# Seven products instead of eight in the first quad of round 1 and of the output

## The chip, the cores and the metric

The kernel runs on one core of one Trainium2 chip. The metric is the device time of the launch in microseconds. The kernel before was timed three times: 909.9, 910.4 and 913.95 us, median 910.4 us. Its profiled execution took 909.45 us by the same clock, and 907.7 us from its first to its last instruction (the span).

## What is computed

One layer of a hybrid decoder, on 2048 tokens of width 1024 with 16 learned tokens ahead of them, in float32 throughout:

```python
hn   = rms_norm(h, norm_g)                        # h: (1, 16 + 2048, 1024)
proj = einsum('bld,de->ble', hn, w_in)            # w_in: 1024 x 4096
cx, cb, cc, cg, q, k, v, rg = split(proj, 8)      # each 512 wide
conv_out = short_conv_branch(cx, cb, cc, conv_w) * silu(cg)      # 3 taps, depthwise
ret  = head_group_norm(retention_chunkwise(rotary(q) * 128**-.5, rotary(k), v), ret_norm_g)
mixed = concat([conv_out, ret * silu(rg)])        # 4 retention heads of 128, chunks of 128
y    = rms_norm(h + einsum('ble,ed->bld', mixed, w_out), final_g)[:, 16:]
```

Nearly all the arithmetic lies in the two projections, `hn @ w_in` and `mixed @ w_out`.

## The kernel before

**Quads.** Both projections are cut into quads: a 2 x 2 grid of 512-deep blocks on one operand by a 2 x 2 grid on the other. The stationary operand of a quad is four 128 x 512 tiles (a pair of 128-column groups of `w_in`, or in the output two 128-token rows of the mixed activations). The moving operand, held in SBUF over many quads, is a 1024 x 1024 matrix in four blocks of 512 x 512: the transposed tokens of one round (`x`, scaled by `norm1_g`), or `w_out`.

A quad is computed in one of two ways. `quad` (matmuls on line 208) forms seven block products in a Strassen-Winograd scheme; it needs seven moving operands, of which numbers 0, 1 and 5 are plain blocks and 2, 3, 4 and 6 are sums of blocks, and seven stationary operands, made from the four raw tiles by four additions on GpSimd (`stationary`). `quad_plain` (matmuls on line 258) forms the eight ordinary block products from the four plain blocks on both sides, with no additions.

**Splits.** A block product takes four 128-deep steps. In each, both float32 operands stand as a high and a low half, and three matmuls of 128 x 512 are issued: low weight by high moving, high by low, high by high. So a block product is 12 matmuls. A split (`split`) is two instructions: ScalarE casts the source to the high half (`mh`, `wh`), VectorE subtracts it from the source for the low half (`ml`, `wl`). `mhIJ` and `mlIJ` are the halves of moving operand I, step J; each has one buffer, so a new round's operand can be written only when the last matmul of the old one has read it. Weight halves go round in three buffers each.

**Rounds.** Tokens run in two rounds of 1024. A round is eight pairs of quads: four retention heads (quads K,V and Q,RG), then four convolution groups (CC,CX and CG,CB). Then the output runs eight quads (`pair`), two 128-token rows each. The moving operand is changed twice: from round 0 to round 1, and from round 1 to `w_out`. These are the two handovers of this document. While a round runs, `prepare` forms the sums for the next operand and stores them in DRAM (`sums_x`, `sums_w`).

**A handover before.** `moving` loads and splits the four plain blocks: 0, 1, 7 and 5, with block 7 in the buffers of operand 4. `plain_parts` splits the four raw weight tiles into the buffers of operand 3. `prepared(m, ..., (1, 3))` reads the sums 2 and 6. The first quad is `quad_plain`; after it `prepared(m, ..., (0, 2))` reads the sums 3 and 4, and the second quad is the first in seven products.

Instructions are issued in order on each engine. A scheduler that plans with a cost model set that order when the kernel was built, across quads; so the queue of an engine mixes the work of the old quad, the handover and the next quad. All DMAs are issued on SyncE.

Of the kernel before, what the change touches and what calls it, by code (L numbers as in the profile page):

```python
# [21 lines left out]
HB = 512  # L22
NR = 2
BLK = SEQ // NR
CH = HB // P
KH = KT // 2
# [7 lines left out]
SUMS = (3, 2, 4, 6)  # L34
# [34 lines left out]
def hybrid_trunk(ctx: ExitStack, tc: tile.TileContext, t, out: bass.AP, chunk_decay):  # L69
# [5 lines left out]
    nc = tc.nc  # L75
# [14 lines left out]
    def gen(name="g"):  # L90
        return sb.tile([P, HB + 16], F32, name=name, tag="g", bufs=GEN)[:, : 2 + HB]
# [96 lines left out]
                nc.sync.dma_start(dst[n, kt], a)  # L188
            yield

    def prepared(m, src, ns):

        for n in ns:
            for kt in range(KH):
                a = gen("t")[:, :HB]
                nc.sync.dma_start(a, src[n, kt])
                parts(m, SUMS[n], kt, a)

    def quad(w, m, take):

# [311 lines left out]
        nc.vector.tensor_tensor(out=a, in0=a, in1=table[:, 0, :], op=ALU.mult)  # L512
        add(nc.vector, a, a, rot[:, :w])

    def head(h, r, m, rot_t, f, blocks, ahead, first=(), between=()):


        between = iter(between)
# [15 lines left out]
        if len(first) > 0:  # L534
            quad_plain(first[0], m, take)
        else:
            quad(stationary(blocks), m, take)
        next(between, lambda: None)()
        q, sg = [None, None], [None, None]

# [14 lines left out]
                nc.scalar.activation(d, d, AF.Silu)  # L555
                sg[j] = d

        if len(first) > 1:
            quad_plain(first[1], m, take)
        else:  # L560
            quad(stationary(load_raw(w_loads(2 * h + 1))), m, take)
# [80 lines left out]
    def output(pair, m, final_g):  # L642
        d = mixed[pair // 2]
        loads = [
            lambda a, i=i, k=k: nc.sync.dma_start(a.rearrange("p (k c) -> p k c", k=KH), d[pair % 2, i, k])
            for i in range(2)
            for k in range(2)
        ]
        ys = [[None, None], [None, None]]
        ss = small.tile([P, 2, 2], F32, name="so", tag="so")  # L650
        for i in range(2):
            for j in range(2):
                y = gen("yo")[:, :HB]
                row = (2 * pair + i) * P
                nc.sync.dma_start(y, x[row : row + P, j * HB : (j + 1) * HB])
                ys[i][j] = y
        last = [None]

        def take(i, j, pp, c):
            y = ys[i][j]  # L660
            if c is not None:
                add(nc.gpsimd, y, y, c)
            last[0] = nc.vector.tensor_tensor(out=y, in0=pp, in1=y, op=ALU.add)  # L663
            junk = sb.tile([P, HB], F32, name="rot", tag="rot", bufs=1)
            nc.scalar.activation(junk, y, AF.Square, accum_out=ss[:, i, j : j + 1])
            if i == j:
                ys[i][j] = gen("z")[:, :HB]
                nc.gpsimd.tensor_tensor(out=ys[i][j], in0=y, in1=final_g[:, j * HB : (j + 1) * HB], op=ALU.mult)

        if pair == 0:  # L670
            w = plain_parts(loads)
            prepared(m, sums_w, (1, 3))
            quad_plain(w, m, take)
            prepared(m, sums_w, (0, 2))
        else:
            quad(stationary(load_raw(loads)), m, take)
        for i in range(2):
# [33 lines left out]
    def ahead(r, n):  # L711


        if n == 2 * NG:
            return None, lambda: None
        blocks = load_raw(w_loads(2 * n))
        if r == 0 and n < NG:
            k, v = meta_state(n, blocks)
            return blocks, lambda: meta_update(n, k, v)
        if r == 0:  # L720
            meta_carry(n - NG, blocks)
        return blocks, lambda: None
# [4 lines left out]
    for r in range(NR):  # L727
# [7 lines left out]
        if r == 0:  # L735
            w = [None] * 4
            loads = w_loads(0)

            def begin(half):
                for n in (half, 2 + half):  # L740
                    w[n] = plain_part(n, loads[n], FIRST_W)

            m, b = moving(
                load_x(r), gain_of, {(0, 0): lambda: begin(0), (0, KH - 1): lambda: begin(1), (0, KT - 1): normalise_meta}
            )
            first = [[p for a, p in w]]
            k0, v0 = meta_state(0, [a for a, p in w])
            first.append(plain_parts(w_loads(1)))
            load_tables()
            nc.sync.dma_start(cols, t["cols"])  # L750
            t3 = [a[:, i * HB : (i + 1) * HB] for a in (row_tile("t3") for _ in range(2)) for i in range(2)]
            t1 = [sb.tile([P, HB], F32, name="t1", tag="tc", bufs=COPIES) for _ in range(KH)]
            for kt in range(KH):
                b11, b21, b12, b22 = (b[n * KH + kt] for n in range(4))
                block_sums(b11, b12, b22, b21, t1[kt], t3[kt], gain_of(kt), gain_of(KH + kt))
                parts(m, 2, kt, b22)
                parts(m, 6, kt, b21)
            for _ in row_factors(0, f):
# [10 lines left out]
            between = (lambda: meta_update(0, k0, v0), rest)  # L769
            later = prepare(load_x(1), sums_x, gain_of)  # L770
        else:
            m, b = moving(load_x(r), gain_of)
            first = [plain_parts(w_loads(0))]
            load_tables()
            prepared(m, sums_x, (1, 3))
            between = (lambda: prepared(m, sums_x, (0, 2)),)
            later = prepare(load_w_out, sums_w)
        blocks = None
        for h in range(NG):
            blocks = head(h, r, m, rot_t, f, blocks, lambda: ahead(r, h + 1), *((first, between) if h == 0 else ()))  # L780
            if h > 0:
                next(later, None)
                next(later, None)
# [3 lines left out]
            for _ in range(3):  # L787
                next(steps, None)

    m, b = moving(load_w_out)  # L790
    final_g = row_tile("final_g")
    nc.sync.dma_start(final_g, t["final_g"].partition_broadcast(P))
    for pair in range(SEQ // (2 * P)):
# [39 lines left out]
```

## Time and profile before

| Engine | busy, us | share of the span | instructions |
|---|---|---|---|
| TensorE (PE), matmuls | 887.2 | 98% | 4407 |
| VectorE (DVE) | 707.1 | 78% | 1177 |
| ScalarE (ACT) | 405.1 | 45% | 807 |
| GpSimd (POOL) | 391.6 | 43% | 290 |

The profiled execution took 909.45 us; its span is 907.7 us, at a mean granted TensorE clock of 0.996. HBM moved 128 GB/s over the span.

In rows of the timeline the first number is the start in us from the begin of the span, the second the length, then engine, line, operation, tiles (out<-in) and shapes, how many were merged, and in brackets the idle time before and what ended it. A row of stretches (windows) gives for each engine its busy time and in brackets how many instructions touch the stretch, then the clock, the DMA share and the rate. Matmuls are pipelined: their rows overlap, so the time of one is read from start to start.

### The profile page before, as it was taken

To read this page: it belongs to the slowest core of one execution; us is meant where nothing else is said; L and a number is where in the kernel's file an instruction comes from. 1 tells how busy PE (TensorE), PEld (TensorE's weight loads), DVE (VectorE), ACT (ScalarE), POOL (GpSimd) and SP (SyncE) were. 2 spreads that over 40 slices of the span, in tenths; PEclk is the share of its full clock that TensorE was granted. 3 is DMA by queue.
4 is the path that set the end of the run, shared out by engine and by line. 5 is a ranking of instruction groups with operands and counts; after the bars stand their busy time and mean duration, and the time that the engine had idled before them with its cause. 6 is when DMAs were issued, how large, how long until landed. Compare 5 with 4: busy or idle time off the path is not lost.

```text
span 907.7 us, 12870 instructions
## 1 busy us (share of the span) xinstructions
PE 887.2 (98%) x4407; PEld 726.4 (80%) x4407; DVE 707.1 (78%) x1177; ACT 405.1 (45%) x807; POOL 391.6 (43%) x290
## 2 busy tenths in 40 slices
PE   8999999999999999999999999999999999999996
PEld 5778878787886777878888888888888888788885
DVE  6699898997665665799888999877767698866764
ACT  8762242424343534565333242433333374554553
POOL 0133142322434645343333323435646554778773
PEclk9999999999999999999999999999999999999999
DMA  9801451623142323564126362222131585555532
GB/s 332 264 3 47 140 163 51 206 82 98 43 149 61 105 82 117 194 236 139 47 67 200 93 204 89 56 59 81 58 93 48 185 284 184 172 183 164 173 108 93
DMA packets 76242, 116.94 MB, mean 129 GB/s; under 512 B 7632, under 2 KB 24336, under 8 KB 76176
## 3 DMA queue, kind: packets, MB, share of 16 engines
q1 hardware_dynamic: 76176, 116.11, 40.0%
q8 instruction: 35, 0.57, 0.3%
q14 instruction: 31, 0.25, 0.1%
HBM read 90.92 MB, written 25.17 MB: 128 GB/s over the span
## 4 chain that ended last, share of the span: by engine, by line
PE 81%; DVE 9%; DMA 3%; ACT 3%; issue 2%; POOL 1%; SPq 0%; POOLq 0%; ACTq 0%; DVEq 0%
PE pj L208 65%; PE pj L258 6%; DVE wl L111 2%; DVE ml L111 1%; PE ms L609 1%; PE ms L610 1%; PE ms L599 1%; DMA ra<-in_x 1%; PE ms L584 1%; PE ms L392 1%; PE ms L633 1%; PE ms L569 1%; PE ms L574 1%; ACT mh L102 1%; DMA ra<-in_w_in 1%
## 5 line engine op out<-in xcount | busy, mean ns | idle before, releaser
L208 PE MATMUL pj<-mh,wl 128*128 128x512 f32 x1008 | 400.6, 398 | 4.8 <-DVE wl L111 3.7
L208 PE MATMUL pj<-ml,wh 128*128 128x512 f32 x1008 | 393.6, 390 | 1.1 <-DVE ml L111 1.1
L208 PE MATMUL pj<-mh,wh 128*128 128x512 f32 x1008 | 393.5, 390 | 0.0
L99 ACT CAST wh<-ra 128x512 fp32r<-128x512 f32 x216 | 133.8, 620 | 306.9 <-PE pj L208 255.3
L208 PEld LDWEIGHTS pj<-mh,wl 128*128 128x128 f32 x1008 | 189.6, 188 | 49.1 <-issue 3.4
L208 PEld LDWEIGHTS pj<-mh,wh 128*128 128x128 f32 x1008 | 189.4, 188 | 39.9
L208 PEld LDWEIGHTS pj<-ml,wh 128*128 128x128 f32 x1008 | 189.8, 188 | 39.0 <-DVE ml L111 1.4
L111 DVE TENSOR_TENSOR wl<-ra,wh 128x512 fp32r<-128x512 f32 x216 | 180.8, 838 | 49.0 <-ACT wh L99 48.4
L111 POOL TENSOR_TENSOR ra<-ra 128x512 f32<-128x512 f32 x72 | 111.9, 1554 | 78.9 <-issue 35.0
L108 POOL TENSOR_TENSOR sa<-ra 128x512 f32<-128x512 f32 x36 | 54.8, 1522 | 119.8 <-DVE wl L111 54.9
L111 POOL TENSOR_TENSOR ra<-sa,ra 128x512 f32<-128x512 f32 x36 | 54.2, 1506 | 107.2 <-DVE wl L111 106.8
L215 ACT COPY tc<-pj 128x512 f32<-128x512 f32 x108 | 62.7, 580 | 0.1
L258 PE MATMUL pj<-mh,ml 128*128 128x512 f32 x128 | 48.6, 394 | 2.6 <-ACT kv L525 1.9
L258 PE MATMUL pj<-ml,mh 128*128 128x512 f32 x128 | 50.2, 392 | 0.1
L258 PE MATMUL pj<-mh,mh 128*128 128x512 f32 x128 | 50.0, 395 | 0.0
L622 POOL TENSOR_TENSOR rp<-rs,neg_half 128x4 f32<-128x4 f32 x16 | 20.5, 1279 | 56.0 <-DVE rs L108 55.7
L467 POOL TENSOR_TENSOR c<-c,tc 128x512 f32<-128x512 f32 x16 | 28.9, 1805 | 34.4 <-ACT tc L490 34.4
L467 POOL TENSOR_TENSOR c<-c,rr 128x512 f32<-128x512 f32 x16 | 30.1, 1879 | 24.8 <-DVE c L455 13.0
L663 DVE TENSOR_TENSOR yo<-pj,yo 128x512 f32<-128x512 f32 x32 | 22.0, 688 | 19.4 <-POOL yo L108 10.1
L111 DVE TENSOR_TENSOR ml<-t,mh 128x512 fp32r<-128x512 f32 x40 | 35.3, 922 | 1.4 <-ACT mh L99 1.4
L108 DVE TENSOR_TENSOR tc<-pj,tc 128x512 f32<-128x512 f32 x32 | 22.0, 686 | 18.0 <-PE pj L208 18.0
L99 ACT CAST wh<-sa 128x512 fp32r<-128x512 f32 x36 | 22.3, 619 | 28.6 <-PE pj L208 28.2
(129 smaller groups left out, 1131.4 us busy)
## 6 DMA issues: line engine op xcount, KB each, us to landing
ra<-in_w_in SPq DMA_DIRECT2D x128, 256.0 KB, 2.7
x<-in_xT SPq DMA_DIRECT2D x48, 256.0 KB, 5.0
ra<-in_x SPq DMA_DIRECT2D x32, 256.0 KB, 3.5
w<-in_w_out SPq DMA_DIRECT2D x32, 256.0 KB, 5.3
ra<-mixed SPq DMA_DIRECT2D x32, 256.0 KB, 2.7
yo<-in_x SPq DMA_DIRECT2D x32, 256.0 KB, 4.3
mixed<-qg SPq DMA_DIRECT2D x16, 256.0 KB, 2.3
sums_x<-x SPq DMA_DIRECT2D x16, 256.0 KB, 2.7
```

The source lines that it names most:

```text
L99: nc.scalar.copy(out=hi, in_=src)
L102: nc.scalar.mul(hi, src, scale)
L108: eng.tensor_tensor(out=out, in0=a, in1=b, op=ALU.add)
L111: eng.tensor_tensor(out=out, in0=a, in1=b, op=ALU.subtract)
L208: nc.tensor.matmul(bank, a[:, ks], b, start=first and kt == 0 and n == 0, stop=kt == KH - 1 and n == 2, skip_group_check=not first,)
L215: nc.scalar.copy(out=c, in_=bank)
L258: nc.tensor.matmul(banks[i], a[:, ks], b, start=half + kt + n == 0, stop=half == 1 and kt == KH - 1 and n == 2,)
L392: nc.tensor.matmul(four[i], meta_s[:, i % 2 * KH + kt, :], blocks[i][:, kt * P : (kt + 1) * P], start=kt == 0, stop=kt == KH - 1,)
L467: eng.tensor_tensor(out=out, in0=a, in1=b, op=ALU.mult)
L569: nc.tensor.transpose(tp[:, c * P : (c + 1) * P], k[j][:, c * P : (c + 1) * P], ident)
L622: nc.gpsimd.tensor_tensor(out=rp, in0=rs, in1=neg_half.rearrange("p (c a) -> p c a", a=1), op=ALU.pow)
L663: last[0] = nc.vector.tensor_tensor(out=y, in0=pp, in1=y, op=ALU.add)
```

## The change

Both handovers run their first quad in `quad`. A new function, `moving_prepared`, loads and splits the seven moving operands in the order 0 to 6, the plain ones from `x` or `w_out` and the sums from DRAM, and calls `stationary` for the quad's weights after operand 1. Block 7 and its four splits are gone, and so are the split weights in the buffers of operand 3 and the split of the reading of sums into two parts. In round 0 the raw weights of the coming quad are loaded ahead by `ahead`. Round 0's own first two quads stay in eight products.

```diff
-    def prepared(m, src, ns):
-
-        for n in ns:
+    def moving_prepared(load, sums, blocks, scale=None):
+
+
+        m = [[] for _ in range(8)]
+        plain = {0: (0, 0), 1: (1, 0), 5: (1, 1)}
+        for i in range(7):
             for kt in range(KH):
-                a = gen("t")[:, :HB]
-                nc.sync.dma_start(a, src[n, kt])
-                parts(m, SUMS[n], kt, a)
+                if i in plain:
+                    half, j = plain[i]
+                    k = half * KH + kt
+                    parts(m, i, kt, load(k, j), scale(k) if scale else None)
+                else:
+                    a = gen("t")[:, :HB]
+                    nc.sync.dma_start(a, sums[SUMS.index(i), kt])
+                    parts(m, i, kt, a)
+            if i == 1:
+                w = stationary(blocks)
+        return m, w
...
-            quad(stationary(blocks), m, take)
+            quad(w or stationary(blocks), m, take)
...
         if pair == 0:
-            w = plain_parts(loads)
-            prepared(m, sums_w, (1, 3))
-            quad_plain(w, m, take)
-            prepared(m, sums_w, (0, 2))
+            m[:], w = moving_prepared(load_w_out, sums_w, load_raw(loads))
+            quad(w, m, take)
...
         if n == 2 * NG:
-            return None, lambda: None
+            return load_raw(w_loads(0)) if r < NR - 1 else None, lambda: None
...
         else:
-            m, b = moving(load_x(r), gain_of)
-            first = [plain_parts(w_loads(0))]
+            m, w = moving_prepared(load_x(r), sums_x, blocks, gain_of)
             load_tables()
-            prepared(m, sums_x, (1, 3))
-            between = (lambda: prepared(m, sums_x, (0, 2)),)
+            first = between = ()
             later = prepare(load_w_out, sums_w)
...
-    m, b = moving(load_w_out)
+    m = []
```

What it does to the queues, at three places. In these rows a line number above 200 is 11 higher in the changed kernel than the same line before.

VectorE, late in the handover to round 1, before the change. `ml` are low halves of moving operands, `wl` low halves of weights; `tc` and `c` belong to the old convolution quad.

```order
L103 SCALAR_TENSOR_TENSOR ml53_3872<-x_3869,gain_69,mh53_3871 128x512
L467 TENSOR_TENSOR tc_3715<-tc_3715,rr_369 128x512
L111 TENSOR_TENSOR ml21_3909<-t_3906,mh21_3908 128x512
L111 TENSOR_TENSOR ml22_3915<-t_3912,mh22_3914 128x512
L111 TENSOR_TENSOR ml23_3921<-t_3918,mh23_3920 128x512
L111 TENSOR_TENSOR wl_4124<-ra_4114,wh_4123 128x512
L111 TENSOR_TENSOR wl_4128<-ra_4116,wh_4127 128x512
L111 TENSOR_TENSOR ml60_3927<-t_3924,mh60_3926 128x512
L467 TENSOR_TENSOR c_3621<-pj_3670,c_3621 128x512
```

And now, about the same place:

```order
L111 TENSOR_TENSOR ml30_3895<-t_3892,mh30_3894 128x512
L111 TENSOR_TENSOR wl_3837<-ra_3776,wh_3836 128x512
L108 TENSOR_TENSOR tc_3715<-pj_3717,tc_3715 128x512
L111 TENSOR_TENSOR ml31_3901<-t_3898,mh31_3900 128x512
L111 TENSOR_TENSOR ml32_3907<-t_3904,mh32_3906 128x512
L111 TENSOR_TENSOR ml33_3913<-t_3910,mh33_3912 128x512
L111 TENSOR_TENSOR wl_3841<-ra_3778,wh_3840 128x512
L111 TENSOR_TENSOR ml40_3919<-t_3916,mh40_3918 128x512
L478 TENSOR_TENSOR c_3621<-pj_3670,c_3621 128x512
```

Before, the first weight split here (`wl_4124`) serves the second new quad. Now the first (`wl_3837`) serves product 0 of the first new quad, and stands behind the splits of moving operands 0, 1, 2 and part of 3.

GpSimd at the same handover, before: the three rows that end the old quad's `c`, and the additions for the second new quad (`sa_4122`, `ra_...`), then those of the third.

```order
L467 TENSOR_TENSOR c_3621<-c_3621,tc_3683 128x512
L467 TENSOR_TENSOR c_3625<-c_3625,rr_369 128x512
L108 TENSOR_TENSOR sa_4122<-ra_4118,ra_4120 128x512
L111 TENSOR_TENSOR ra_4118<-ra_4114,ra_4118 128x512
L467 TENSOR_TENSOR c_3625<-c_3625,tc_3715 128x512
L111 TENSOR_TENSOR ra_4114<-sa_4122,ra_4114 128x512
L111 TENSOR_TENSOR ra_4116<-ra_4116,ra_4114 128x512
L108 TENSOR_TENSOR sa_4414<-ra_4273,ra_4275 128x512
```

And now:

```order
L108 TENSOR_TENSOR sa_3835<-ra_3780,ra_3782 128x512
L111 TENSOR_TENSOR ra_3780<-ra_3776,ra_3780 128x512
L478 TENSOR_TENSOR c_3621<-c_3621,tc_3683 128x512
L478 TENSOR_TENSOR c_3625<-c_3625,rr_369 128x512
L111 TENSOR_TENSOR ra_3776<-sa_3835,ra_3776 128x512
L111 TENSOR_TENSOR ra_3778<-ra_3778,ra_3776 128x512
L478 TENSOR_TENSOR c_3625<-c_3625,tc_3715 128x512
L108 TENSOR_TENSOR sa_4108<-ra_4104,ra_4106 128x512
```

The four additions in the handover are now those of the first new quad, and the second new quad's four (from `sa_4108`) follow behind them: four more in all.

GpSimd at the handover to the output, before (`yo` and `z` are the output's residual rows, `c` the old quad's):

```order
L467 TENSOR_TENSOR c_6857<-c_6857,tc_6947 128x512
L111 TENSOR_TENSOR ra_7382<-sa_7390,ra_7382 128x512
L111 TENSOR_TENSOR ra_7384<-ra_7384,ra_7382 128x512
L668 TENSOR_TENSOR z_7242<-yo_7109,final_g_7106 128x512
L668 TENSOR_TENSOR z_7303<-yo_7115,final_g_7106 128x512
L274 TENSOR_TENSOR rf_7355<-rs_v_7356,neg_half_72 128x1
```

And now:

```order
L111 TENSOR_TENSOR ra_7007<-sa_7063,ra_7007 128x512
L111 TENSOR_TENSOR ra_7009<-ra_7009,ra_7007 128x512
L108 TENSOR_TENSOR yo_6999<-yo_6999,tc_7229 128x512
L478 TENSOR_TENSOR c_6843<-c_6843,tc_6933 128x512
L679 TENSOR_TENSOR z_7248<-yo_6999,final_g_6996 128x512
L108 TENSOR_TENSOR sa_7365<-ra_7361,ra_7363 128x512
L108 TENSOR_TENSOR yo_7001<-yo_7001,tc_7262 128x512
L111 TENSOR_TENSOR ra_7361<-ra_7357,ra_7361 128x512
L108 TENSOR_TENSOR yo_7005<-yo_7005,tc_7277 128x512
L111 TENSOR_TENSOR ra_7357<-sa_7365,ra_7357 128x512
```

The first output quad now adds parts of products to the residual rows on GpSimd (three `yo` rows, which eight products did not need), and the additions for the second output quad stand between them.

More of the change, by code (lines that the diff above doesn't have):

```diff
@@ L513, in rotary, with head @@
         add(nc.vector, a, a, rot[:, :w])
-    def head(h, r, m, rot_t, f, blocks, ahead, first=(), between=()):
+    def head(h, r, m, rot_t, f, blocks, ahead, w=None, first=(), between=()):
         between = iter(between)
@@ L556, in take @@
                 sg[j] = d
-        if len(first) > 1:
+        if first:
             quad_plain(first[1], m, take)
@@ L769, in hybrid_trunk @@
             between = (lambda: meta_update(0, k0, v0), rest)
+            blocks = None
             later = prepare(load_x(1), sums_x, gain_of)
         else:
-            m, b = moving(load_x(r), gain_of)
-            first = [plain_parts(w_loads(0))]
+            m, w = moving_prepared(load_x(r), sums_x, blocks, gain_of)
             load_tables()
-            prepared(m, sums_x, (1, 3))
-            between = (lambda: prepared(m, sums_x, (0, 2)),)
+            first = between = ()
             later = prepare(load_w_out, sums_w)
-        blocks = None
         for h in range(NG):
-            blocks = head(h, r, m, rot_t, f, blocks, lambda: ahead(r, h + 1), *((first, between) if h == 0 else ()))
+            blocks = head(h, r, m, rot_t, f, blocks, lambda: ahead(r, h + 1), *((w, first, between) if h == 0 else ()))
             if h > 0:
```

## The prediction

> **What bounds the kernel now.** First the page's busy times, and its 40 slices for TensorE and VectorE, in tenths.
>
> ```profile
> PE 887.2 (98%) x4407; PEld 726.4 (80%) x4407; DVE 707.1 (78%) x1177; ACT 405.1 (45%) x807; POOL 391.6 (43%) x290
> ...
> PE   8999999999999999999999999999999999999996
> ...
> DVE  6699898997665665799888999877767698866764
> ```
>
> TensorE (PE) is busy from end to end, so over the whole kernel work taken from it is time won. But a VectorE share of 78% is an average: slices 18 and 19, and 33, read 9, and there the handovers lie. The stretches show it: the two handovers' splits, then a stretch of the output for comparison.
>
> ```profile
> 380.50:413.50 33.00, 32.40 (x144) 26.49 (x143) 33.00 (x42) 21.80 (x39) 15.36 (x8) 1.00 0.65 243
> 728.60:759.20 30.60, 30.53 (x135) 24.96 (x134) 30.60 (x42) 19.11 (x36) 17.38 (x8) 1.00 0.70 223
> ...
> 806.00:826.00 20.00, 20.00 (x90) 16.57 (x89) 12.07 (x18) 9.89 (x21) 14.72 (x13) 1.00 0.50 159
> ```
>
> The fourth group is VectorE: 33.00 of 33.00 us and 30.60 of 30.60, against 12.07 of 20 later. In both handovers VectorE is full without a gap, and TensorE just is not held up, because eight plain products need only half of the moving operands.
>
> **The price of a product.** TensorE's first quad in round 1 runs without a break from here to here:
>
> ```profile
> 395.98 0.39 PE L258 MATMUL pj<-ml,mh 128*128 128x512 f32 x1
> 396.20 0.39 PE L208 MATMUL pj<-mh,wl 128*128 128x512 f32 x1
> ...
> 398.92 0.39 PE L258 MATMUL pj<-mh,mh 128*128 128x512 f32 x1
> ...
> 416.60 0.39 PE L258 MATMUL pj<-mh,mh 128*128 128x512 f32 x1
> 416.83 0.39 PE L208 MATMUL pj<-mh,wl 128*128 128x512 f32 x1
> ```
>
> From 398.92 to 416.60 are 79 matmuls, the first and the last of them included: 17.68 / 78 = 0.227 us each, start to start, not the 0.39 that a row shows. A product of 12 costs 2.72 us, and two products are taken out: **5.4 us**, if TensorE stays fed. 17 matmuls of that quad ran ahead of the old one's last 12 (from 396.20), so without them the old quad ends at 398.92 - 17 x 0.227 = 395.1. From there the new quad needs the halves of operand and weight k at 395.1 + 2.72 k.
>
> **What VectorE takes.** Two rows give its pace when nothing disturbs it, one when something does, and the last ends the handover's splits:
>
> ```profile
> 380.50 2.44 DVE L103 SCALAR_TENSOR_TENSOR ml<-x,gain,mh 128x512 fp32r<-128x512 f32 x2
> 385.99 2.07 DVE L103 SCALAR_TENSOR_TENSOR ml<-x,gain,mh 128x512 fp32r<-128x512 f32 x3
> 390.26 1.88 DVE L111 TENSOR_TENSOR ml<-ra,mh 128x512 fp32r<-128x512 f32 x3
> 408.38 4.58 DVE L111 TENSOR_TENSOR ml<-t,mh 128x512 fp32r<-128x512 f32 x3
> 412.88 0.68 DVE L111 TENSOR_TENSOR wl<-ra,wh 128x512 fp32r<-128x512 f32 x1
> ```
>
> Three splits take 1.88 us, so 0.60 from start to start (1.88 less one of 0.68, halved), or 0.665 with the gain; the three at 408.38 take 4.58. What lies beside those is GpSimd:
>
> ```profile
> 379.39 2.34 POOL L467 TENSOR_TENSOR c<-c,rr 128x512 f32<-128x512 f32 x1 [1.36 <-DVE c L455]
> 388.07 1.72 POOL L467 TENSOR_TENSOR c<-c,tc 128x512 f32<-128x512 f32 x1 [6.34 <-ACT tc L490]
> 396.02 1.74 POOL L467 TENSOR_TENSOR c<-c,rr 128x512 f32<-128x512 f32 x1 [6.23 <-DVE c L467]
> 397.73 1.74 POOL L108 TENSOR_TENSOR sa<-ra 128x512 f32<-128x512 f32 x1
> 399.55 1.62 POOL L111 TENSOR_TENSOR ra<-ra 128x512 f32<-128x512 f32 x1
> 404.99 4.02 POOL L467 TENSOR_TENSOR c<-c,tc 128x512 f32<-128x512 f32 x1 [3.82 <-ACT tc L490]
> 408.97 1.73 POOL L111 TENSOR_TENSOR ra<-sa,ra 128x512 f32<-128x512 f32 x1
> 410.79 1.63 POOL L111 TENSOR_TENSOR ra<-ra 128x512 f32<-128x512 f32 x1
> ```
>
> The view of one tile, the low halves made from read sums, gives the shortest, the median and the longest split of the whole kernel in ns:
>
> ```profile
> L111 DVE TENSOR_TENSOR ml<-t,mh x40: 677/684/1783, 48.3 to 778.8; 128x512 fp32r<-128x512 f32 x40
> ```
>
> A split lasts 684 ns in the median and at most 1783: a GpSimd operation can hold it up by 1.1 us. From 380.50 to 412.96 are 40 VectorE instructions (42 touch the stretch, one at each edge): 24 x 0.60 + 16 x 0.665 = 25.0 us, and they took 32.5. The 7.4 us over fall to 8 GpSimd rows, **0.9 us each**. In the output's handover 40 instructions from 728.61 to 759.20 took 30.6 us for 24.0, again beside 8: 0.82.
>
> ```profile
> 728.61 1.28 DVE L111 TENSOR_TENSOR ml<-w,mh 128x512 fp32r<-128x512 f32 x2
> ...
> 753.90 5.30 DVE L111 TENSOR_TENSOR ml<-t,mh 128x512 fp32r<-128x512 f32 x6
> ```
>
> [...]
>
> [...]
>
> [...]
>
> **The change, part by part.** Removed at each handover: 12 matmuls, four splits of block 7, four of weights. Added: seven splits of weights. So VectorE has about as many instructions; ScalarE (21.80 of 33.00 us busy) covers its half of them and goes at nothing. SyncE's queue loses the four loads of block 7 at each handover; the four raw weight tiles go ahead of the moving blocks, in round 0 by `ahead`, and the sums 2 to 4 and 6 are read in one run instead of two. The rate over the same 33 us, slice by slice:
>
> ```profile
> GB/s 400 405 410 405 405 407 395 392 412 385 392 390 400 405 397 412 405 410 395 365 382 340 243 25 0 0 0 37 278 2 0 0 0 10 0 0 177 328 151 0
> ```
>
> At 405 GB/s a tile of 262,144 bytes takes 0.65 us, no more than VectorE's own pace, and the transfers ran out at 400 us, 13 us before VectorE's last split: they lead. So the DMAs go at nothing; were a sum late, its four tiles would come 4 x 0.65 = 2.6 us later. What changes is when VectorE's work is due, and that GpSimd has four additions more ahead of it.
>
> Round 1. In the changed order the low half of weight k is instruction 21, 26, 33, 36, 41, 45 and 48 after 380.50, with all of operand k's first steps before it; and 4, 6, 7, 7, 8, 8, 8 GpSimd operations are due by then (old `c` rows and the new additions, of which two must follow weights 0 and 1, whose tiles they overwrite). With 0.60 an instruction, 0.065 more for each gain split and 0.9 an addition, weight 0 is ready at 380.5 + 12.6 + 0.5 + 3.6 = 397.2, 2.1 late. Weight 1: 402.0, 2.1 behind the shifted 399.9. Weight 2: 407.1, 2.4 behind. Weight 3 in time, weight 4 0.5 behind, the rest in time. Stalls: **7.1 us**.
>
> Output. TensorE's rows there, with the stalls that end in them:
>
> ```profile
> 736.63 0.39 PE L208 MATMUL pj<-mh,wh 128*128 128x512 f32 x1
> 737.09 0.50 PE L258 MATMUL pj<-mh,ml 128*128 128x512 f32 x1
> ...
> 746.54 0.39 PE L258 MATMUL pj<-mh,mh 128*128 128x512 f32 x1
> ...
> 775.13 0.39 PE L208 MATMUL pj<-mh,wh 128*128 128x512 f32 x1
> 776.10 0.47 PE L208 MATMUL pj<-mh,wl 128*128 128x512 f32 x1 [0.58 <-DVE wl L111]
> 777.68 0.50 PE L208 MATMUL pj<-ml,wh 128*128 128x512 f32 x1 [1.12 <-DVE ml L111]
> ```
>
> At 746.54 the plain quad goes on behind the old one's last product; 17 of its matmuls ran ahead here too, so the old quad ends at 746.54 - 17 x 0.227 = 742.7. The low halves are instruction 17, 21, 27, 31, 36, 40 after 728.6, and for the next quad's product 0, which TensorE's order puts before product 6, instruction 47. GpSimd operations due: 4, 5, 6, 7, 9, 11, 13, since the `yo`, `z` and the second quad's additions now come in between. At 0.85 each the waits are 0, 0, 1.7, 0.5, 2.0, 1.4 and 3.2: **8.8 us**.
>
> What the stalls of before come to there, from start to start over 0.227: 0.23 at 737.09, 0.74 at 776.10 and 1.35 at 777.68: 2.3 us, for sums 3 and 4 split late, which are now split earlier: won.
>
> The sum: -5.4 - 2.3 + 7.1 + 8.8 = **+8.2 us** on the profiled execution's 909.45, so 917.65; taken as **917.5**. The median of the runs, 910.4, is 0.95 above that execution, within their spread.
>
> **The one unknown price** is what a GpSimd operation costs here. From below: at nothing, weight 2 of round 1 is 0.3 late, nothing else, and the sum is -5.4 - 2.3 + 0.3 = -7.4: 902. From above: at 1.1 each the same chains give 8.7 + 12.1, and +13.1: 922.5. At 0.5 they give 3.9 + 4.3, and +0.5. I take 0.9 and 0.85, measured in the very stretches that the change alters.
>
> **Rivals.**
>
> *VectorE is kept ahead, and the 5.4 us are won.* GpSimd's operations would have to wait for VectorE instead. Two rows are like that, 404.99 with 4.02 us, and this one:
>
> ```profile
> 734.96 5.03 POOL L467 TENSOR_TENSOR c<-c,tc 128x512 f32<-128x512 f32 x1 [3.90 <-ACT tc L490]
> ```
>
> There a run of splits went by while GpSimd stood. Against it: the other rows of 1.6 to 1.75 show GpSimd let in at the next split, and weights 2 to 6 are made from what it delivers. Price 0 to 0.3: 902 to 906.
>
> *A draw.* The additions fall half into waits that VectorE has anyway, for instance behind products whose results it takes. Price about 0.5: 908 to 913. For it: the stalls themselves make gaps in which GpSimd costs nothing. Against it: VectorE's queue was never empty in 33 us.
>
> *GpSimd becomes the bound of the first output quads.* Its stretch 806 to 826 is busy 14.72 of 20 already, and three `yo` rows and a full set of additions now come while it also ends the convolution. Should the second quad's weights be late too, by another 1.7 us for each of three operations, it is 5 more: 923 and over. It decides when the second output quad's weight 2, not its low halves, ends TensorE's wait.
>
> *That the change does not do what it says* is out: the order has 24 matmuls fewer on line 208 and 258 together.
>
> **How the numbers follow.** A difference under 0.5% (4.6 us) cannot be told from none here. VectorE bound as summed: 0.61, at 914 to 922, of which 0.04 lies within 0.5%. Won in full: 0.18. A draw: 0.15. GpSimd bound: 0.06. So faster 0.18, same 0.19, slower 0.63. The range reaches to both sides until about 0.2 is out: 905 to 923.
>
> **What would show it.** In the profile after: matmuls with line 219 in both handovers, waiting for `wl` or `ml`, some 7 us in the first 30 us of round 1 and 8 to 9 around the first two output quads; VectorE full in both; more low halves near 1.78 us. The forecast is wrong if TensorE runs through both handovers, or if what it waits for there is a DMA or ScalarE rather than VectorE.

## The result and the profile after

The changed kernel takes 923.4 us (median; 921.2 to 924.3), the kernel before beside it 910.9 us: the ratio is 1.0131, with a 95% interval of 1.0112 to 1.0150. So it is 12.5 us slower; the forecast was 8.2 us and 917.5. The time lies 0.4 us above the top of the stated range. The profiled execution has a span of 922.2 us, 14.5 more than the one of before.

The page's busy times after:

```profile
PE 887.3 (96%) x4383; PEld 723.1 (78%) x4383; DVE 704.2 (76%) x1178; ACT 407.1 (44%) x808; POOL 400.8 (43%) x301
```

The 24 matmuls are gone, VectorE has as many instructions as ever, and GpSimd has 11 more. The view of the stretches, for the handover to round 1 and for the output's:

```profile
380.50:413.50 33.00, 26.28 (x103) 19.76 (x102) 33.00 (x42) 23.12 (x42) 15.96 (x10) 0.95 0.73 254
740.00:785.00 45.00, 35.66 (x144) 27.24 (x143) 43.40 (x51) 27.77 (x55) 26.18 (x17) 0.96 0.65 206
```

In the first stretch VectorE is busy for 33.00 of 33.00 us with 42 instructions, exactly as before, and in the second for 43.40 of 45.00. What has changed is TensorE: 26.28 us of work instead of 32.40. And a column that read 1.00 before reads 0.95 and 0.96: the granted clock.

TensorE's own rows show both. The row where a product begins carries the wait in brackets; the rows behind two of the waits start 0.43 us apart instead of 0.23:

```profile
397.52 0.50 PE L219 MATMUL pj<-mh,wl 128*128 128x512 f32 x1 [0.60 <-DVE wl L111]
402.12 0.50 PE L219 MATMUL pj<-mh,wl 128*128 128x512 f32 x1 [1.58 <-DVE wl L111]
...
404.75 0.39 PE L219 MATMUL pj<-mh,wh 128*128 128x512 f32 x1
408.01 0.65 PE L219 MATMUL pj<-mh,wl 128*128 128x512 f32 x1 [2.87 <-DVE wl L111]
408.46 0.63 PE L219 MATMUL pj<-ml,wh 128*128 128x512 f32 x1
...
411.44 0.45 PE L219 MATMUL pj<-mh,wh 128*128 128x512 f32 x1
411.73 0.39 PE L219 MATMUL pj<-mh,wl 128*128 128x512 f32 x1
...
754.41 0.50 PE L219 MATMUL pj<-mh,wl 128*128 128x512 f32 x1 [0.99 <-DVE wl L111]
760.28 0.77 PE L219 MATMUL pj<-mh,wl 128*128 128x512 f32 x1 [2.85 <-DVE wl L111]
...
763.28 0.40 PE L219 MATMUL pj<-ml,wh 128*128 128x512 f32 x1
...
768.96 0.47 PE L219 MATMUL pj<-mh,wl 128*128 128x512 f32 x1 [1.64 <-DVE wl L111]
774.63 0.47 PE L219 MATMUL pj<-mh,wl 128*128 128x512 f32 x1 [2.71 <-DVE wl L111]
778.75 0.50 PE L219 MATMUL pj<-mh,wl 128*128 128x512 f32 x1 [1.12 <-DVE wl L111]
```

All eight waits end with a low half of weights from VectorE. A wait costs some 0.16 us more than its bracket says, since rows overlap: 408.01 less 404.75, less the normal 0.227, is 3.03 us. So products 0, 1 and 2 of round 1 lost 0.76, 1.75 and 3.03, 5.5 us in all, and the output's products 1, 2, 4, 5 and the next quad's 0 lost 1.15, 3.01, 1.80, 2.87 and 1.28, 10.1 us. Which product it is follows from the operand in TensorE's order. The slow rows come on top: 8 steps from 408.01 to 411.44 take 3.43 us instead of 1.82, and 7 steps from 760.28 to 763.28 take 3.00 instead of 1.59, 3.0 us together.

How a low half comes to be late is seen in the timeline of all engines ahead of 408.01:

```profile
405.72 1.59 POOL L478 TENSOR_TENSOR c<-c,tc 128x512 f32<-128x512 f32 x1 [1.90 <-ACT tc L501]
...
406.11 1.75 DVE L111 TENSOR_TENSOR wl<-ra,wh 128x512 fp32r<-128x512 f32 x1
...
408.01 0.65 PE L219 MATMUL pj<-mh,wl 128*128 128x512 f32 x1 [2.87 <-DVE wl L111]
```

The split starts 0.39 us after a GpSimd product and takes 1.75 us instead of 0.68; TensorE starts 0.15 us behind its end.

### The profile page after: what moved, and what is told of

Same layout as the page of the kernel before. It is cut to its first block, busy times and chain, and to the rows that moved or that the text cites. A ratio compares the mean times of both kernels' runs of the same rounds, so it can differ in the third digit from the quotient of the medians.

```text
span 922.2 us, 12850 instructions
## 1 busy us (share of the span) xinstructions
PE 887.3 (96%) x4383; PEld 723.1 (78%) x4383; DVE 704.2 (76%) x1178; ACT 407.1 (44%) x808; POOL 400.8 (43%) x301
## 4 chain that ended last, share of the span: by engine, by line
PE 79%; DVE 9%; ACT 4%; DMA 4%; issue 3%; POOL 1%; SPq 0%; POOLq 0%; DVEq 0%; ACTq 0%
PE pj L219 68%; DVE ml L111 2%; PE pj L269 2%; DVE wl L111 2%; DMA ra<-in_x 1%; PE ms L620 1%; PE ms L621 1%; PE ms L610 1%; ACT mh L102 1%; PE ms L595 1%; DMA ra<-in_w_in 1%; PE ms L403 1%; PE ms L644 1%; PE ms L580 1%; PE ms L585 1%
## 5 line engine op out<-in xcount | busy, mean ns | idle before, releaser
L219 PE MATMUL pj<-mh,wl 128*128 128x512 f32 x1064 | 424.9, 399 | 20.5 <-DVE wl L111 17.3
L219 PE MATMUL pj<-ml,wh 128*128 128x512 f32 x1064 | 416.5, 391 | 0.0
L219 PE MATMUL pj<-mh,wh 128*128 128x512 f32 x1064 | 416.5, 391 | 0.0
L219 PEld LDWEIGHTS pj<-mh,wl 128*128 128x128 f32 x1064 | 200.8, 189 | 70.7 <-ACT mh L99 8.7
L111 DVE TENSOR_TENSOR wl<-ra,wh 128x512 fp32r<-128x512 f32 x228 | 194.0, 852 | 53.6 <-ACT wh L99 53.2
L219 PEld LDWEIGHTS pj<-mh,wh 128*128 128x128 f32 x1064 | 200.6, 189 | 42.8
L219 PEld LDWEIGHTS pj<-ml,wh 128*128 128x128 f32 x1064 | 200.9, 189 | 39.9 <-issue 0.5
L633 POOL TENSOR_TENSOR rp<-rs,neg_half 128x4 f32<-128x4 f32 x16 | 20.5, 1280 | 56.2 <-DVE rs L108 56.0
L108 POOL TENSOR_TENSOR yo<-yo,tc 128x512 f32<-128x512 f32 x24 | 37.7, 1570 | 10.6 <-ACT tc L226 10.6
L679 POOL TENSOR_TENSOR z<-yo,final_g 128x512 f32<-128x512 f32 x16 | 26.9, 1683 | 11.4 <-DVE yo L674 11.4
L637 DVE TENSOR_SCALAR pm<-ms,mv,rp 128x128 f32<-128x128 f32 x64 | 21.9, 404 | 12.9 <-POOL rp L633 12.9
```

Source lines behind the costliest of these rows:

```text
L108: eng.tensor_tensor(out=out, in0=a, in1=b, op=ALU.add)
L111: eng.tensor_tensor(out=out, in0=a, in1=b, op=ALU.subtract)
L219: nc.tensor.matmul(bank, a[:, ks], b, start=first and kt == 0 and n == 0, stop=kt == KH - 1 and n == 2, skip_group_check=not first,)
L633: nc.gpsimd.tensor_tensor(out=rp, in0=rs, in1=neg_half.rearrange("p (c a) -> p c a", a=1), op=ALU.pow)
L637: nc.vector.tensor_scalar(out=y[:, cs], in0=o[:, cs], scalar1=mv[:, c, 0:1], scalar2=rp[:, c, :], op0=ALU.subtract, op1=ALU.mult,)
```

## The experiments

**Theory 1** is the prediction's: VectorE has no gap, and each GpSimd operation on SBUF tiles takes about 0.85 us from it. **Theory 2**: VectorE has too many instructions in that order, whatever GpSimd does. **Theory 3**: the weights' sums themselves come late out of GpSimd's queue, and VectorE is only the last to pass them on.

### One handover at a time

Round 1 with seven products, the output as before (the other kernel is the reverse):

```diff
-            m[:], w = moving_prepared(load_w_out, sums_w, load_raw(loads))
-            quad(w, m, take)
+            w = plain_parts(loads)
+            prepared(m, sums_w, (1, 3))
+            quad_plain(w, m, take)
+            prepared(m, sums_w, (0, 2))
```

> The first quad of round 1 runs in seven products as in the changed kernel, the first quad of the output in eight as before. The profiles put some 6.5 us of the changed kernel's 14.5 us longer span at the handover to round 1 and 7.9 at the output. If the two handovers lose independently, this kernel takes before + 6 to 7, so 916.5 to 918. If one place alone is at fault (the output, say, with what round 1 loses made good later), it is at 911 or at 923.

> The other half: the output's first quad in seven products, round 1 begins in eight as before. Independent losses: before + 7 to 8 less nothing, so 917 to 919, and the differences of this kernel and of the one with round 1 alone add up to the whole change's 12.5. One place alone: 911 or 923.

Round 1 alone: 917.4 us, ratio 1.0072 (1.0049 to 1.0096). The output alone: 917.1 us, ratio 1.0070 (1.0053 to 1.0088). Beside 910.8 us these are +6.6 and +6.4; their sum, 13.0, is the whole change's 12.5 within the intervals. Each handover loses for itself, and neither of them is worth doing this way.

### The additions taken out, and run for nothing

The first kernel has no additions for the two handover quads:

```diff
-                w = stationary(blocks)
+                w = bare(blocks)        # seven splits of the four raw tiles
```

> Left out of the computation: the four additions on GpSimd for the weights of the two handover quads; their seven splits are made from the four raw tiles, so that VectorE and ScalarE have the same number of instructions in nearly the same order. Theory 1 (a GpSimd operation takes 0.85 us from VectorE, which has no gap): 4 x 0.85 = 3.4 us less lateness at each handover, and with the stalls below 2 us TensorE's clock does not fall behind them (2.0 and 1.6 us): some 10 us less, 913. Theory 2 (VectorE's own count of instructions and their order makes the splits late): no change, 922 to 924. Theory 3 (the sums come late from GpSimd, whose own queue waits): as theory 1, 912 to 914.

The second kernel keeps GpSimd's four operations per handover, in time and size, but nobody reads what they make:

```diff
+        add(nc.gpsimd, s1, a21, a22)
+        sub(nc.gpsimd, s1, a11, a21)
+        sub(nc.gpsimd, s1, w[0][1].bitcast(F32), a21)
+        sub(nc.gpsimd, s1, w[1][1].bitcast(F32), a21)
+        return w + [parts(a) for a in (a11, a21, a21, a12, a22)]
```

> Left out of the computation: the results of the same eight additions. GpSimd still does four per handover, of the same size, the first two ready when the raw tiles have landed, the last two after the low halves of weights 0 and 1, as in the changed kernel, but into a tile that nobody reads; the seven splits are made from the raw tiles. VectorE's order is that of the changed kernel. Theory 1 (VectorE is held up while GpSimd runs): as the changed kernel, 921 to 924. Theory 3 (the sums come late): as without the additions, about 913. Theory 2 (VectorE's own count): 922 to 924, but then the kernel without additions is there too.

Without the additions: 915.8 us, ratio 1.0057 (1.0042 to 1.0073). With additions that nobody reads: 923.5 us, ratio 1.0148 (1.0131 to 1.0165), the changed kernel's time. This settles theory 3: late sums are not the cause, since here no split waits for one. The group of the products' first matmuls says the same in one line each; behind the bar stand busy time, the mean of one, and the idle time ahead of the group. Before:

```profile
L208 PE MATMUL pj<-mh,wl 128*128 128x512 f32 x1008 | 400.6, 398 | 4.8 <-DVE wl L111 3.7
```

After:

```profile
L219 PE MATMUL pj<-mh,wl 128*128 128x512 f32 x1064 | 424.9, 399 | 20.5 <-DVE wl L111 17.3
```

Without the additions, and with additions for nothing:

```profile
L231 PE MATMUL pj<-mh,wl 128*128 128x512 f32 x1064 | 424.2, 399 | 15.7 <-DVE wl L111 13.9 <-DVE yo L686 1.2 <-ACT tc L238 0.6
```

```profile
L237 PE MATMUL pj<-mh,wl 128*128 128x512 f32 x1064 | 425.2, 400 | 19.8 <-DVE wl L111 14.7 <-ACT mh L99 2.2 <-ACT tc L244 1.6
```

Idle time ahead of products: 4.8, 20.5, 15.7, 19.8 us. But 915.8 was above the 913 expected, and still 5 us above before, so a good part of the waiting was left. Theory 2 could live in that part.

### GpSimd kept out of the handovers altogether

```diff
-                mul(nc.gpsimd, cs[j], cs[j], rr[j])
-                mul(nc.gpsimd, cs[j], cs[j], c)
+                if g < NG - 1:
+                    mul(nc.gpsimd, cs[j], cs[j], rr[j])
+                    mul(nc.gpsimd, cs[j], cs[j], c)
...
-            if c is not None:
+            if c is not None and pair > 0:
                 add(nc.gpsimd, y, y, c)
```

and the second new quad's additions left out like the first one's.

> Left out of the computation, beside the additions for the two handover quads' weights: all else that GpSimd does in the handovers, that is the two products for the old convolution quad's c (last group of each round), the additions for the second new quad's weights, the three additions of parts to the first output quad's residual rows, and its gain (a copy on ScalarE in its place). VectorE's splits and their order stay. Theory 1 (what GpSimd takes from VectorE is all that makes the splits late): by the sum of the prediction with GpSimd at nothing the splits are 0.3 us late, so 5.4 us of products and 2.3 us of old stalls are won: 903 to 905. Theory 2 (VectorE's count and order are the rest of it): the 4.9 us that the kernel without the eight additions still stands above before stay, 913 to 916.

904.5 us, ratio 0.9940 (0.9918 to 0.9962): inside the 903 to 905 of theory 1, and at the prediction's lower bound of 902 but for 2.5 us. VectorE's instructions in the handovers are the same splits in nearly the same order. The stretches and the group:

```profile
380.50:413.50 33.00, 31.07 (x134) 24.48 (x133) 32.34 (x53) 25.32 (x45) 0.00 (x0) 1.00 0.79 283
728.60:775.00 46.40, 45.19 (x198) 36.83 (x198) 40.36 (x63) 34.97 (x69) 9.13 (x7) 1.00 0.72 256
```

```profile
L231 PE MATMUL pj<-mh,wl 128*128 128x512 f32 x1064 | 422.8, 398 | 6.9 <-DVE wl L111 4.2 <-ACT tc L238 1.7 <-ACT wh L99 0.9
```

VectorE does 53 instructions in the 33 us in which it did 42 before and after the change, and still has 0.66 us to spare; TensorE's clock is at 1.00. In the second stretch GpSimd's 9.13 us begin at 761.17, with the second output quad. Theory 2 falls: without GpSimd VectorE feeds the seven products. What this kernel leaves out is work of the layer, so its time is not one that the layer could have.

### The costs by themselves

A kernel that computes nothing of the layer runs the disputed pieces one after the other, each stretch kept apart from the next; in short form:

```diff
+    both(24, a)             # VectorE alone: lo = a - b
+    both(24, a); gps(8)     # beside eight GpSimd additions
+    # 24 subtractions, and 3 GpSimd additions of results 2, 8 and 14
+    both(24, bank); gps(8)  # a in PSUM
+    one_in(24); gps(8)      # tensor_scalar, one SBUF input
+    # then matmuls with rests of 1 to 6 ScalarE copies
```

> Not this computation at all: the disputed costs by themselves, in stretches that are separated from each other. VectorE's subtraction of two SBUF tiles alone, GpSimd's addition alone, both side by side with GpSimd's eight back to back, VectorE with three single GpSimd additions, VectorE with one input in PSUM beside GpSimd, VectorE with one SBUF input beside GpSimd; then matmuls with rests of 1 to 6 ScalarE copies, once and five times in a row. Theory 1: 24 subtractions alone take 14.5 us (0.60 each), beside three single additions some 2.5 us more (0.85 each), with PSUM or one input no more than alone. Against it would be 14.5 us in all of these. On the clock: if it takes one rest of some 2.8 us, only the long rests are followed by matmuls of 0.43 us; if short rests in a row do it as well, the runs with five rests of 1.2 to 2.4 us show them too.

The timeline of VectorE, one row a stretch:

```profile
6.71 14.54 DVE L40 TENSOR_TENSOR lo<-a,b 128x512 fp32r<-128x512 f32 x24 [6.71 <-SPq L51]
31.33 23.06 DVE L40 TENSOR_TENSOR lo<-a,b 128x512 fp32r<-128x512 f32 x24 [10.07 <-SPq L55]
54.44 17.74 DVE L61 TENSOR_TENSOR wide<-a,b 128x512 fp32r<-128x512 f32 x24
72.34 14.44 DVE L40 TENSOR_TENSOR lo<-bank,b 128x512 fp32r<-128x512 f32 x24 [0.15 <-SPq L64]
86.92 16.66 DVE L44 TENSOR_SCALAR lo<-a 128x512 fp32r<-128x512 f32 x24
```

and GpSimd's in its first two:

```profile
21.38 9.80 POOL L48 TENSOR_TENSOR so<-c,d 128x512 f32<-128x512 f32 x8 [20.94 <-SPq L53]
31.37 13.44 POOL L48 TENSOR_TENSOR so<-c,d 128x512 f32<-128x512 f32 x8 [0.19 <-SPq L55]
```

Alone 24 subtractions take 14.54 us. Eight GpSimd additions beside them add (23.06 - 14.54) / 8 = 1.07 us each, and three single ones (17.74 - 14.54) / 3 = 1.07. With one input in PSUM the 24 take 14.44 us beside eight additions, no longer than the SBUF form alone; that form was not run without GpSimd. So the price per operation is 1.07 us where it meets a subtraction of SBUF tiles. The prediction took 0.85 to 0.9 from the kernel; that some operations there met another kind of instruction would explain the difference, but it is not shown. GpSimd pays too: its eight additions take 13.44 us instead of 9.80.

A GpSimd addition alone takes 9.80 / 8 = 1.22 us here, and VectorE loses 1.07 us to it, nearly its whole length.

### Work made ahead

GpSimd's additions for the handover quads were moved several quads earlier, with their results stored and read as raw tiles. This kernel and the five below compute the whole layer.

```diff
+            if h == NG - 1:
+                sum_ahead(*((mixed_loads(0), first_w) if r else (w_loads(0), first_x)))
```

> The whole computation, in the changed kernel's way, but the four sums of the weights of each handover quad are formed by GpSimd several quads earlier (after the last head of the round), stored, and read as raw tiles in the handover. That is the kernel without the eight additions (915.8) as a correct one, with eight tiles more to store and to read: theory 1 expects 914 to 917, and the same stalls in the handovers. If the additions cost as much where they are done now, it is back at 921 to 924.

913.7 us beside 908.8, ratio 1.0056 (1.0041 to 1.0071): the same ratio as without the additions. Earlier, they cost nothing that can be seen.

Next, the moving sums were stored as split halves, and read straight into the operands' buffers.

```diff
...
-                    parts(m, i, kt, a)
...
+                    nc.sync.dma_start(hi.bitcast(F32), sums[SUMS.index(i), kt, 0])
+                    nc.sync.dma_start(lo.bitcast(F32), sums[SUMS.index(i), kt, 1])
```

> The whole computation. While a round runs, the sums for the next moving operand are not only formed but also split, and both halves are stored; in the handover the halves of operands 2, 3, 4 and 6 are read straight into their buffers. That takes 16 of VectorE's some 47 instructions out of each handover (16 x 0.60 = 9.6 us) and puts them where VectorE has gaps; GpSimd's work stays. If VectorE is what binds, with or without GpSimd, its lateness of 2 to 6 us from product 2 on is gone, the first two products stay some 2 us late together: 911 - 5.4 - 2.3 + 2 x 2 = 907, between 904 and 909. Rival: the transfers bind, since a handover now reads 12 + 32 + 4 tiles of 0.65 us, 31 us, and each read of a half stands in the queue until the old quad leaves its buffer: 912 to 918.

> As the kernel that stores the sums' halves (922), with the sums formed and split beside the convolution groups instead of the heads, and operand 5 split ahead of operand 4. In that kernel the handovers were nearly free of stalls, and TensorE lost some 8 us in the rounds instead, waiting for VectorE beside the heads, where it is nearly full. If that is the reason, those 8 us go, and 912 to 914 is left; a stall or two fewer at operand 5 may take it to 909. If the extra work costs the same wherever it lies, 920 to 923.

> Both: the halves of the moving sums and the weights' sums of the two handover quads are made ahead, beside the convolution groups. VectorE then has 16 instructions fewer in each handover and GpSimd four fewer. Theory 1: the handovers run without stalls of more than 1 us each, 911 - 5.4 - 2.3 = 903, with some 2 to 4 us for the first two products and for the work in the rounds: 904 to 909. If the work beside the convolution groups makes TensorE wait there, 912 or more.

All three came out slower than before, far from the 904 to 914 us hoped for: 922.0, 926.1 and 926.2 us, ratios 1.0114, 1.0185 and 1.0183. Of the expectations' second branches (912 to 918, 920 to 923, 912 or more) only the last covers its time. The handovers did as expected: the first new quads' waits shrank. The rounds did not. Beside the heads and beside the convolution groups alike, TensorE waits for VectorE where it did not before, or not as long; a row of the first kernel and one of the second:

```profile
564.70 0.79 PE L224 MATMUL pj<-mh,wl 128*128 128x512 f32 x1 [2.46 <-DVE kv L108]
```

```profile
273.82 0.26 PE L444 MATMUL ms<-ident,mk 16*128 16x16 f32 x1 [4.27 <-DVE mk L442]
```

A likely reason, argued and not shown apart, is that sixteen more splits in a stretch of the rounds meet chains in which TensorE waits for VectorE within a few us, and VectorE's average of 76% says nothing of those. TensorE's clock has its part: up to the last matmul, the granted clock falls to one half in four places of the first trace, four of the second and three of the third, against one place before; its mean over each trace is 0.991, 0.990 and 0.988, against 0.996. Whether a finer spreading would do it was not tried.

The last pair keeps to what worked. In the first kernel the weights' sums of the second quads are made ahead as well; in the second, the old convolution quad's four products for `c`, in the last group of each round, also go from GpSimd to VectorE.

```diff
-                mul(nc.gpsimd, cs[j], cs[j], rr[j])
-                mul(nc.gpsimd, cs[j], cs[j], c)
+                eng = nc.gpsimd if g < NG - 1 else nc.vector
+                mul(eng, cs[j], cs[j], rr[j])
+                mul(eng, cs[j], cs[j], c)
```

> The whole computation. As the kernel with the weights' sums of each handover quad made ahead (913.7), and the same for the second quad of each, so that GpSimd's last work in the handovers is the old convolution quad's two products for each c, the residual rows and their gain. The second quad's additions fall partly into the handover when the first quad's are gone: theory 1 expects up to 2 us less, 911 to 914.

> As the kernel before it in this list, with the four products for c of each round's last convolution group on VectorE instead of GpSimd. VectorE gets four instructions more in each handover, 4 x 0.60 = 2.4 us. Theory 1 with the price measured apart (1.07 us taken from VectorE by one GpSimd operation): 4 x (1.07 - 0.60) = 1.9 us less per handover although VectorE has more to do, 0 to 4 us faster than its neighbour, 907 to 912, level with before or a little faster. Theory 2 (VectorE's count binds): up to 4.8 us slower than its neighbour, 915 to 919.

With the products on GpSimd: 912.8 us, ratio 1.0026 (1.0008 to 1.0045). With them on VectorE: **908.6 us, ratio 0.9974 (0.9957 to 0.9990)**, 2.1 us faster than before. VectorE was given eight instructions more and the kernel became 4.2 us faster: no count of VectorE's instructions explains that, and it is the clearest sign for theory 1. The same two stretches, first with the products on GpSimd, then on VectorE:

```profile
375.00:415.00 40.00, 37.59 (x160) 29.12 (x158) 39.16 (x57) 28.91 (x51) 12.11 (x8) 1.00 0.81 282
740.00:785.00 45.00, 41.78 (x175) 33.44 (x174) 40.75 (x52) 26.94 (x53) 22.91 (x15) 0.96 0.70 233
```

```profile
375.00:415.00 40.00, 37.88 (x162) 29.77 (x161) 39.89 (x65) 28.35 (x51) 1.31 (x3) 1.00 0.81 288
740.00:785.00 45.00, 42.03 (x183) 33.89 (x182) 39.52 (x55) 26.98 (x55) 26.94 (x16) 1.00 0.73 236
```

VectorE gets 65 instructions done in 40 us instead of 57, and in the output TensorE's clock stays at 1.00. Part of the 4.2 us is that clock: over the runs of each kernel its mean is 0.9945 and 0.9963, a difference of 0.0018 or some 1.6 us of 910. That it follows from the shorter waits alone is not shown.

## Why the prediction was right, and where it failed

**The bound and the sign** held; the time did not, since 923.4 lies outside the range. VectorE fills both handovers, the new waits sit where they were forecast, and they end with VectorE's low halves. The three rivals fell: VectorE is not kept ahead, the additions do not fall into waits that are there anyway (taking them out gives 7.6 us), and GpSimd's queue is not what is waited for (additions for nothing cost as much). That this last rival was given 923 us and over, the time that was measured, is chance.

**The gain of two products**, 5.4 us, was not measured by itself. Without GpSimd in the handovers the kernel is 5.7 us faster than before, which fits it; but GpSimd's work is left out there too, and by the prediction's sum it would have been 7.4.

**The chain of splits**, instruction by instruction: weights 0, 1 and 2 of round 1 were put at 397.2, 402.0 and 407.1; the products began at 397.52, 402.12 and 408.01. The waits were forecast at 7.1 and 8.8 us, 15.9 together, and came to 5.5 and 10.1, 15.6 together. That the sum came out is luck, since the errors cancel: single waits were off by up to 1.9 us. The output's waits began a product earlier than forecast, and product 0 of round 1 waited 0.76 and not 2.1, because the old quad itself ended later, behind a wait at its product 5 that grew. That product's row before, and after:

```profile
389.49 0.50 PE L208 MATMUL pj<-mh,wl 128*128 128x512 f32 x1 [0.60 <-ACT tc L215]
```

```profile
390.04 0.68 DVE L111 TENSOR_TENSOR wl<-ra,wh 128x512 fp32r<-128x512 f32 x1
390.86 0.47 PE L219 MATMUL pj<-mh,wl 128*128 128x512 f32 x1 [1.59 <-ACT mh L99]
```

The bracket names ScalarE. But the tile named is a moving half of the new quad, which the old one does not read, and a split of the old quad's weights ended on VectorE at 390.04 + 0.68 = 390.72, 0.14 us ahead of the matmul, as at 408.01. In the kernel with additions for nothing the same place waits 1.00 us, and there the bracket names `wl` on VectorE. So it is most likely VectorE once more, already late within the old quad, where the prediction's chains do not look.

**The step that failed** is the sum: it prices the waits and sets what comes behind them at nothing, without a reason. Two of the eight waits were followed by matmuls at half speed, for 3.4 and 3.0 us, and 1.6 and 1.4 us were lost. The terms as they were measured: -5.4 - 2.3 + 15.6 + 3.0 for the clock + 1.0 for the old quad's wait = +11.9. They come from the profiled execution, whose span is 14.5 us longer; the medians differ by 12.5. Of the 2.6 us that are left, 0.9 is a wait for ScalarE in the middle of round 1, at 703.57, which before does not have, and most of the rest is delays of 0.25 us and less around the waits.

Nor does a higher price per operation do it. At 1.1 us, near the 1.07 measured apart, the prediction's chains give 922.5, close to the measured time, but by way of 20.8 us of waits where 15.6 were seen.

The profile of before had the effect of the clock, in a place that the change does not touch; a wait, and behind it matmuls at 0.42 to 0.58 us from start to start:

```profile
121.31 0.48 PE L420 MATMUL ms<-mk 16*128 16x128 f32 x2 [2.13 <-DVE mk L108]
...
123.34 0.78 PE L208 MATMUL pj<-mh,wl 128*128 128x512 f32 x1
123.92 0.63 PE L208 MATMUL pj<-ml,wh 128*128 128x512 f32 x1
124.34 0.63 PE L208 MATMUL pj<-mh,wh 128*128 128x512 f32 x1
```

TensorE ran at half speed behind this wait of 2.13 us and behind those of 2.87 and 2.85 us in the changed kernel, so whoever forecasts new waits of that length has to price what comes behind them.

## What to carry to other kernels

An engine that is full without a gap can have a price list for its neighbours: here one GpSimd operation on SBUF tiles cost VectorE, at subtractions of two SBUF tiles, 1.07 us, more than the 0.60 of such a subtraction, and with eight products moved from GpSimd to VectorE the kernel took 908.6 us instead of 912.8. Before an edit moves due times closer together, write down for each operand the instruction number at which it is ready and add the neighbours' price; that found seven of the eight waiting products here, each wait to within 2 us. Then allow for half speed behind a wait that leaves TensorE idle for most of 3.4 us (1.6 and 1.4 us were lost behind two of the eight here), and if an edit loses, look for what can leave the tight stretch, not only for what can be undone.

## What the hardware showed that was not expected

**Half speed behind waits, by a grid and not by one length.** In the kernel of pieces, 40 matmuls behind a rest of 1.38, 2.03, 2.68 and 3.33 us, then 12 behind rests of 1.38 and of 2.03 us in a row:

```profile
130.52 9.37 PE L76 MATMUL acc<-m,w 128*128 128x512 f32 x40 [1.38 <-ACT m L81]
141.92 9.37 PE L76 MATMUL acc<-m,w 128*128 128x512 f32 x40 [2.03 <-ACT m L81]
153.96 10.96 PE L76 MATMUL acc<-m,w 128*128 128x512 f32 x40 [2.68 <-ACT m L81]
168.25 10.89 PE L76 MATMUL acc<-m,w 128*128 128x512 f32 x40 [3.33 <-ACT m L81]
...
228.70 3.02 PE L76 MATMUL acc<-m,w 128*128 128x512 f32 x12 [1.38 <-ACT m L81]
...
269.60 4.61 PE L76 MATMUL acc<-m,w 128*128 128x512 f32 x12 [2.03 <-ACT m L81]
```

A single rest of 2.03 us costs nothing behind it, one of 2.68 us costs 1.6; but rests of 2.03 us with 3 us of work between them cost 1.6 us each (4.61 against 3.02). In the layer's kernels the length alone does not decide it either. The wait of 2.13 us at 121.31 has slow rows behind it before; the same wait in the kernel with round 1 alone, at 120.83, has none.

The granted clock in the traces shows the pattern. It falls to one half for 3.41 us at a time, at times for two or three such stretches in a row, and within a trace all of them lie on one grid: in the changed kernel they begin at 121.41, 408.13 and 759.70 us, 84 and 103 times 3.413 us apart. In the stretch of the grid ahead of each one TensorE was busy for at most 2.13 of 3.41 us, mostly for far less: for 1.28, 0.54 and 1.14 us in the changed kernel. Three of the grid in the changed kernel; the clock is the column ahead of the last two:

```profile
404.72:408.13 3.41, 0.54 (x3) 0.15 (x2) 3.41 (x5) 3.12 (x6) 1.59 (x1) 1.00 0.10 29
408.13:411.54 3.41, 3.41 (x9) 2.63 (x10) 3.41 (x6) 0.10 (x1) 0.46 (x1) 0.50 0.60 154
411.54:414.96 3.42, 3.42 (x17) 2.80 (x16) 3.42 (x4) 1.11 (x2) 2.46 (x2) 1.00 0.00 0
```

A wait is shared out between the stretches of the grid that it touches. In the kernel without additions a wait of 3.03 us, up to 757.50, falls half into one and half into the next, and nothing follows; in the one with round 1 alone two waits of 0.42 and 0.73 us fall into one, and half speed follows at 785.50:

```profile
752.67:756.09 3.42, 1.81 (x8) 1.15 (x7) 3.42 (x3) 2.78 (x6) 3.42 (x3) 1.00 0.57 171
756.09:759.50 3.41, 2.00 (x9) 1.66 (x10) 3.41 (x5) 0.81 (x3) 0.98 (x2) 1.00 0.31 102
```

```profile
782.09:785.50 3.41, 2.10 (x8) 1.16 (x8) 3.41 (x4) 1.17 (x3) 2.20 (x2) 1.00 0.35 115
```

Over all the traces here, between the first 8 us and the last matmul (in the kernel of pieces from its first matmul on), each of the 35 stretches with TensorE busy for 1.50 us or less was followed by half speed, and none with 2.14 us or more; in the changed kernel and the one before the followed ones had 0.54, 1.14 and twice 1.28 us, and the next, 1.77, had nothing behind it. Of the 46 in between six were, so the busy time of one stretch does not settle it all. Where the grid begins differs from trace to trace: counted back in steps of 3.4133 us, 1.94 us into the span in the changed kernel, 2.23 before, 1.74 without the additions, 0.43 with round 1 alone. The waits of 2.87 and 2.85 us in the changed kernel cost 1.6 and 1.4 us more, its wait of 2.71 us and the one of 3.03 us without the additions nothing, so what a wait of some 3 us costs is in part luck.

**One SBUF input did not spare VectorE here.** In the kernel of pieces the last VectorE row, `tensor_scalar` on one SBUF tile, takes 16.66 us for 24 beside eight GpSimd additions. These ended at 98.27 us, and from there on it goes like this:

```profile
98.81 4.78 DVE L44 TENSOR_SCALAR lo<-a 128x512 fp32r<-128x512 f32 x14
```

That is 0.34 us each, 8.2 for 24, so the eight additions took (16.66 - 8.2) / 8 = 1.06 us each here too; the input in PSUM was the only form tried that was left alone. With 0.34 us instead of 0.60 this is also the faster form; one with a single SBUF input at the slower pace was not run.
